# Eight ScalarE split copies put behind attention's exponentials, and a norm broadcast put into an earlier matmul group, in a two-layer decoder trunk

## The chip, the cores and the metric

The kernel runs on one core of a Trainium2 chip. The metric is the device time in microseconds (us) of one execution. The profile page and the trace describe one execution of their own; its time stands beside its span in the table below.

## The reference

The kernel computes two identical layers over 512 tokens of width 1024, in float32. Cut to what the change touches:

```python
def hybrid_layer(x, ...):                       # DEPTH = 2, SEQ = 512, D_MODEL = 1024
    h = rmsnorm(x, norm_mix)                    # one factor per token, then a gain per column
    z = h @ w_in
    q_a, k_a, v_a, q_m, k_m, v_m, o_m, if_m, gates = jnp.split(z, splits, axis=-1)
    # branch A: 8 query heads over 2 key heads of 64, blocks of 128 queries, window 128
    q_a, k_a = rope(rmsnorm(q_a)), rope(rmsnorm(k_a))
    att = sliding_window_attention(q_a, k_a, v_a, att_sinks)
    # branch B: mLSTM, 4 heads, q and k of 64, v of 128, in chunks, with running maximum
    hm = sigmoid(o_m) * rmsnorm(mlstm_chunkwise(q_m, k_m, v_m, i_pre, f_pre))
    mixed = sigmoid(gA) * (att @ w_att_branch) + sigmoid(gB) * (hm @ w_m_branch)
    x = x + mixed @ w_out
    u = relu(rmsnorm(x, norm_ffn) @ w_ff1)
    return x + (u * u) @ w_ff2
```

## The kernel before

**Matmuls.** Every large product is made of three matmuls (`mm3`, L47 issues each): an operand is split into a high part `h` and a low part `l`, and `h*h`, `h*l` and `l*h` are added in PSUM. Activations (`i` in the trace) are split once. Weights come in chunks of 128 x 512: a DMA on SP's queue into one of three raw buffers (`w`), a ScalarE copy into `wh` (L192), a VectorE subtraction into `wl` (L193), in four buffers each. A *group* is 512 output columns: 8 chunks (the depth 1024) times 4 blocks of 128 times 3 matmuls, 96 in all, into four PSUM banks, `mm`, which come as two pairs (blocks 0 and 1; blocks 2 and 3) out of six banks that go round. After its last chunk a group is evacuated out of PSUM, bank by bank. The matmuls of 128x128 on 128x512 that read `i` and `wh` or `wl` are "group matmuls" below.

**The remaining two banks**, `aux`, serve all small matmuls one after the other: transposes (L51), attention's scores and outputs (L47), and the broadcast of the norm factor. A small matmul that needs an `aux` bank can start when the readers of that bank's previous contents are done.

**The order.** `weave(fill, side)` writes a program order: `fill` is a list of matmul steps, a group being 8 units wide, and each entry of `side` is a function that is called at a place in those units. A scheduler then orders the instructions of each engine, by priority and by when it believes them ready. Each engine runs its own instructions strictly in that order.

The mixer has two weaves. The first holds the group of attention's q (units 0 to 8) and that of k, v and the i and f logits (8 to 16, 264 columns wide, "the key group"). The second holds the mLSTM's q and k (0 to 8), two gate groups g0 and g1 (8 to 24, evacuated by L761, a VectorE multiplication by the norm row), the mLSTM's v (24 to 32), and others behind it. Attention hangs in it as eight *units* (query block, key head), numbered 0 to 7; unit n begins at 5.75 + 1.65 n. Each has:

- scores: two small groups of matmuls from `kT` and `t`, read by a ScalarE copy of the previous block's half (L653) and by VectorE (L654);
- softmax: VectorE's maximum (L665 to L668), four ScalarE exponentials (L671) and the one of the sink, `es` (L673), VectorE's sum, reciprocal and scaling (L674 to L676);
- the probabilities' turn: four transposes (L51), the split in ScalarE and VectorE (L204, L205), and two POOL masks of each half (L690, L692);
- the output: four matmuls `aux<-t,v`, a ScalarE copy (L704), two VectorE sums (L708), and the split of the result (L711, L712).

For every query block, `q_tr` turns q and splits it in four ScalarE copies (L632) and four VectorE subtractions (L633). The mLSTM's decay runs beside it: the transposes of `acol`, the scans (L525, L528), and the copies of `cm` (L533, L534).

**`qk_split`** (L728 and on) splits the mLSTM's q and k into high and low parts, eight calls at 12.5 + 1.4 n: a ScalarE copy of 64 x 512 (L732 in the profile), then for q a POOL cast and memset and a VectorE subtraction (L737), for k a VectorE subtraction (L740). The results (`m_q`, `m_ql`, `m_k`) are used by `m_weights`, behind the v group.

**`Norm.along`** makes the row of norm factors `row[0]`, 128 x 512, each factor over all partitions: four VectorE multiplications of the identity by a column (L329), one float32 matmul with a matrix of ones into an `aux` bank (`aux<-t,ones` in the trace), and a ScalarE copy (L333). `norm.columns` (at 6.9 of the first weave) makes the column; `along` is called at 1.5 of the second weave. The mLSTM's q and k are multiplied by the row when they are evacuated.

`tc.issue_after(X)` makes the scheduler place what stands inside it behind X.

Of the kernel before, what the change touches and what calls it, by code (L numbers as in the profile page):

```python
# [12 lines left out]
AF = mybir.ActivationFunctionType  # L13
# [22 lines left out]
def hybrid_kernel(ctx, tc, x, norm_mix, w_in, att_q_norm, att_k_norm, att_sinks, m_gate_bias,  # L36
# [3 lines left out]
    ve, sc, gp = nc.vector, nc.scalar, nc.gpsimd  # L40
# [32 lines left out]
    def slot(dt=F32, shape=(P, T)):  # L73
        return now["act"].tile(list(shape), dt, tag="a", name=nm("a"))
# [19 lines left out]
    def f32(ap):  # L94
        return ap.bitcast(F32)
# [19 lines left out]
    def gains(row, c0):  # L115
        n = row.shape[0]
        gps = aux([P, n])
        pe.transpose(gps, row, ident[:n, :n])
        ve.tensor_copy(gcol[:, c0:c0 + n], gps)

    def g_mix(l, k):
        return gcol[:, 8 * l + k:8 * l + k + 1]

    def g_ffn(l, k):
        return gcol[:, 16 + 8 * l + k:17 + 8 * l + k]
# [214 lines left out]
    norm = norm0 = Norm(lambda k: g_mix(0, k))  # L340
# [89 lines left out]
    def mixer(l, norm, late, order, phase):  # L430
# [24 lines left out]
        row = []  # L455
# [4 lines left out]
        def ev_kv(b, ps):  # L460
# [2 lines left out]
        weave(tok_steps(acts, wcols(C_Q, 512), ev_q, order=order)  # L463
              + tok_steps(acts, lambda k: [W[k * P:(k + 1) * P, C_K:C_K + 256],
                                           W[k * P:(k + 1) * P, C_IF:C_IF + 8]], ev_kv, width=264),
              late + [(6.9, norm.columns)])


        ig = sm([P, NB, MH], "ig", 1)
# [113 lines left out]
        last_exp = []  # L583
# [31 lines left out]
        def q_vec(b):  # L615
            rope(q_tok[b].rearrange("p (h d) -> p h d", d=HD), b, HQ)

        def q_tr(b):


            ps = aux()
            for j in range(4):
                pe.transpose(ps[:, j * P:(j + 1) * P], q_tok[b][:, j * P:(j + 1) * P], ident)
            for j in range(2):
                qT[b, j] = temp(F32R)
                t4 = qT[b, j].rearrange("p (n i t) -> p n i t", n=2, i=2)
                p4 = ps[:, 2 * j * P:2 * (j + 1) * P].rearrange("p (n t) -> p n t", n=2)
                for i in range(2):
                    r = slice(64 * i, 64 * i + 64)
                    o = slice(64 - 64 * i, 128 - 64 * i)  # L630
                    g = gcols[0][r, l:l + 1]
                    sc.activation(t4[r, :, i, :], p4[r], AF.Copy, scale=g)  # L632
                    ve.scalar_tensor_tensor(t4[o, :, i, :], p4[r], g, f32(t4[r, :, i, :]), op0=ALU.mult,  # L633
                                            op1=ALU.subtract)
# [93 lines left out]
        def qk_split(m, i):  # L728
            t = qk_raw[m]
            r, o = slice(64 * i, 64 * i + 64), slice(64 - 64 * i, 128 - 64 * i)  # L730
            d = slot(F32R)
            sc.activation(d[r], t[r], AF.Copy)  # L732
            if m < 2:
                gp.tensor_copy(d[o], f32(d[r]))
                low = slot(F32R)
                gp.memset(f32(low[o]), 0.0)
                ve.tensor_tensor(low[r], t[r], f32(d[r]), op=ALU.subtract)  # L737
                m_q[2 * m + i], m_ql[2 * m + i] = d, low
            else:
                ve.tensor_tensor(d[o], t[r], f32(d[r]), op=ALU.subtract)  # L740
                m_k[2 * (m - 2) + i] = d
# [27 lines left out]
        def ev_v(b, ps):  # L769
            if b == 0:  # L770
# [7 lines left out]
        side = [(0, lambda: q_vec(0)), (0, k_vec), (0, lambda: q_vec(1)),  # L778
                (first - 1.25, k_tr), (first - 1.75, lambda: q_tr(0))]
        for i, (b, kv) in enumerate(units):  # L780
# [6 lines left out]
            if kv == 0 and b + 1 < NB:  # L787
                if b + 2 < NB:
                    side.append((at + 1, lambda b=b: q_vec(b + 2)))
                side.append((at + 2 * apart - 1.75, lambda b=b: q_tr(b + 1)))  # L790
        side.append((1.5, lambda: row.append(norm.along())))
        side += [(8.45 + 3.0 * i, f) for i, f in enumerate((gating0, gating1, gating2, gating3))]
        side += [(12.5 + 1.4 * n, lambda n=n: qk_split(n // 2, n % 2)) for n in range(8)]
        g0, s0 = gate_steps(0)
        g1, s1 = gate_steps(1)
# [104 lines left out]
        norm = Norm(lambda k: g_ffn(l, k))  # L900
# [10 lines left out]
    def mlp(l, norm, late, phase):  # L911
# [355 lines left out]
        def go(i, s, n):  # L1267
# [16 lines left out]
    late = ([(0.75 + 0.9 * (k - 2), lambda k=k: norm.turn(k)) for k in range(2, KT)]  # L1284
            + [(6.5, lambda: gains(grow, 16))]
            + [(3.0 + 2.0 * j, lambda j=j: norm.squares(j)) for j in range(2)])
    order = None
    for l in range(DEPTH):
        with ExitStack() as phase:
            norm = mixer(l, norm, late, order, phase)  # L1290
        late = norm.steps(1, 1.5, 0.5)
        with ExitStack() as phase:
            norm = mlp(l, norm, late, phase)
        late = norm.steps(0, 1.5, 0.5) if norm else []
        order = LATE_FIRST
# [40 lines left out]
```

## Time and profile before

| | |
|---|---|
| median of 3 runs | 1312.2 us (1311.24 to 1312.83) |
| the profiled execution's own time | 1312.1 us |
| its span in the trace | 1310.4 us, mean granted TensorE clock 0.998 |
| TensorE (PE) | 1288.5 us busy, 98% of the span, 7126 matmuls |
| VectorE (DVE) | 961.9 us, 73% |
| ScalarE (ACT) | 771.2 us, 59% |
| GpSimd (POOL) | 214.6 us, 16% |
| DMA | 196.52 MB, 171 GB/s of HBM traffic over the span |

1.7 us of the profiled execution lie outside its span. Matmul durations overlap, since the next one starts while the last one drains: what a group matmul takes of TensorE is the distance of two starts, not the duration shown. In the timeline, an entry in square brackets is idle time of that engine just before the instruction, and what ended it; `x2` or `x4` joins equal instructions that follow each other.

### The profile page before, as it was taken

What the parts mean: (1) busy time and instruction counts of PE and PEld (TensorE: products, weight loads), DVE (VectorE), ACT (ScalarE), POOL (GpSimd) and SP (SyncE); (2) the same over time, 40 slices, a digit from 0 to 9 for tenths busy, and PEclk for the clock granted to TensorE, in tenths of its full rate; (3) what the DMA queues carried; (4) which work ended last, traced back from release to release, by engine and by line L of the source; (5) the groups of instructions that cost most, each with busy time, mean ns of one, the idle gap of its engine ahead of it and who ended that gap; (6) DMA issues with size and microseconds to landing.
All of it is one profiled execution on the core that took longest, in us unless ns stands there. A gap on an engine that the chain in (4) does not pass through costs nothing.

```text
span 1310.4 us, 19489 instructions
## 1 busy us (share of the span) xinstructions
PE 1288.5 (98%) x7126; PEld 1111.5 (85%) x7126; DVE 961.9 (73%) x1477; ACT 771.2 (59%) x1365; POOL 214.6 (16%) x303
## 2 busy tenths in 40 slices
PE   9999999999999999999999999999999999999998
PEld 7877788888899989999887777888888999999987
DVE  4689755466587897978946896645766888979786
ACT  5556755444475666667544667554444766666663
POOL 4502201100011122120014122011000111212100
PEclk9999999999999999999999999999999999999999
DMA  5322236738288999787313222367392799897743
GB/s 153 102 68 67 64 91 162 183 112 221 78 205 192 266 185 238 180 182 197 112 37 109 65 65 73 107 159 169 121 263 50 194 232 247 176 260 150 188 139 136
DMA packets 139169, 196.52 MB, mean 150 GB/s; under 512 B 10424, under 2 KB 76576, under 8 KB 139072
## 3 DMA queue, kind: packets, MB, share of 16 engines
q1 hardware_dynamic: 93040, 135.88, 33.6%
q0 software_dynamic: 37568, 44.17, 21.9%
q10 hardware_dynamic: 8464, 15.21, 3.8%
q8 instruction: 56, 0.92, 0.3%
q14 instruction: 41, 0.34, 0.1%
HBM read 193.14 MB, written 31.46 MB: 171 GB/s over the span
## 4 chain that ended last, share of the span: by engine, by line
PE 86%; DVE 6%; ACT 4%; DMA 2%; issue 2%; SPq 0%; ACTq 0%; DVEq 0%; POOLq 0%
PE mm L47 74%; PE aux L47 10%; PE aux L51 2%; DMA raw<-in_w_ff_dram 1%; ACT wh L192 1%; DVE wl L193 1%; DMA w<-in_w_in_dram 1%; ACT t L671 1%; DVE t L633 0%; DVE a L740 0%; DVE t L676 0%; ACT t L632 0%; DVE wl L942 0%; ACT wh L938 0%; DVE u L956 0%
## 5 line engine op out<-in xcount | busy, mean ns | idle before, releaser
L47 PE MATMUL mm<-i,wh 128*128 128x512 f32 (+1 forms) x1216 | 329.8, 357 | 0.0
L938 ACT ACTIVATE wh<-raw 128x1024 fp32r<-128x1024 f32 x218 | 229.4, 1056 | 136.0 <-PE mm L47 68.2
L942 DVE TENSOR_TENSOR wl<-raw,wh 128x1024 fp32r<-128x1024 f32 x218 | 264.4, 1221 | 59.7 <-ACT wh L938 58.3
L193 DVE TENSOR_TENSOR wl<-w,wh 128x512 fp32r<-128x512 f32 (+1 forms) x208 | 140.1, 675 | 128.8 <-ACT wh L192 121.0
L47 PEld LDWEIGHTS mm<-i,wh 128*128 128x128 f32 x1216 | 210.5, 190 | 25.9 <-issue 0.5
L192 ACT ACTIVATE wh<-w 128x512 fp32r<-128x512 f32 (+1 forms) x208 | 127.0, 612 | 149.0 <-PE mm L47 122.9
L47 PE MATMUL mm<-i,wl 128*128 128x512 f32 (+1 forms) x608 | 214.3, 352 | 0.0
L47 PE MATMUL mm<-wh,uh 128*128 128x512 f32 x448 | 175.0, 391 | 0.0
L47 PE MATMUL mm<-wl,uh 128*128 128x512 f32 x448 | 174.7, 390 | 0.0
L47 PE MATMUL mm<-wh,ul 128*128 128x512 f32 x448 | 174.3, 389 | 0.0
L982 POOL DMA_DIRECT2D raw<-in_w_ff_dram x56 | 72.7, 1298 | 496.2 <-DVE wl L942 326.5
L47 PE MATMUL mm<-wh,i 128*128 128x512 f32 (+1 forms) x512 | 149.2, 368 | 1.0 <-ACT wh L192 0.7
L47 PEld LDWEIGHTS mm<-i,wl 128*128 128x128 f32 x608 | 115.4, 190 | 15.4 <-issue 0.5
L47 PE MATMUL mm<-hs,wh 128*128 128x256 f32 x672 | 122.2, 283 | 0.7 <-ACT u L1173 0.7
L47 PEld LDWEIGHTS mm<-hs,wh 128*128 128x128 f32 x672 | 105.7, 192 | 2.2 <-ACT u L1173 1.1
L47 PEld LDWEIGHTS mm<-wh,i 128*128 128x128 f32 x512 | 91.7, 188 | 17.1 <-DVE i L208 1.1
L47 PEld LDWEIGHTS mm<-wh,ul 128*128 128x128 f32 x448 | 84.1, 188 | 17.8
L47 PEld LDWEIGHTS mm<-wh,uh 128*128 128x128 f32 x448 | 84.3, 188 | 16.5
L47 PEld LDWEIGHTS mm<-wl,uh 128*128 128x128 f32 x448 | 84.2, 188 | 16.0
L47 PE MATMUL mm<-hs,wl 128*128 128x256 f32 x336 | 95.1, 283 | 0.0
L47 PE MATMUL mm<-wl,i 128*128 128x512 f32 (+1 forms) x256 | 93.1, 364 | 0.0
L996 DVE SCALAR_TENSOR_TENSOR x<-mm,ninv,x 128x512 f32<-128x512 f32 x112 | 81.0, 745 | 10.2 <-PE mm L47 10.0
(245 smaller groups left out, 2164.5 us busy)
## 6 DMA issues: line engine op xcount, KB each, us to landing
raw<-in_w_ff_dram SPq DMA_DIRECT2D x124, 512.0 KB, 5.9
w<-in_w_in_dram SPq DMA_DIRECT2D x128, 256.0 KB, 2.7
raw<-in_w_ff_dram POOLq DMA_DIRECT2D x56, 512.0 KB, 7.7
sum<-in_w_ff_dram ACTq DMA_DIRECT2D x28, 512.0 KB, 5.3
raw<-sum SPq DMA_DIRECT2D x28, 512.0 KB, 4.3
sum<-in_w_ff_dram POOLq DMA_DIRECT2D x20, 512.0 KB, 6.3
w<-in_w_out_dram SPq DMA_DIRECT2D x32, 256.0 KB, 3.3
w<-in_w_att_branch_dram SPq DMA_DIRECT2D x16, 256.0 KB, 2.6
```

The lines of the kernel that those rows point to most:

```text
L47: return nc.tensor.matmul(*args, **kw)
L51: return nc.tensor.transpose(*args)
L192: last_wh[:] = sc.activation(wh[:, :off], raw[:, :off], AF.Copy), wh
L193: ve.tensor_tensor(wl[:, :off], raw[:, :off], f32(wh[:, :off]), op=ALU.subtract)
L671: sc.activation(s3[:, i, :], s3[:, i, :], AF.Exp, bias=m[:, i:i + 1], accum_out=den[:, i:i + 1])
L938: last_wh[:] = sc.activation(hi, r, AF.Copy), hi[:, 0, :]
L942: ve.tensor_tensor(lo, r, f32(hi), op=ALU.subtract)
L982: nc.gpsimd.dma_start(r, w1_block(k, n, c0), accum_op=ALU.add)
L996: ve.scalar_tensor_tensor(xh[:, i, :], ps[i], norm.inv[:, 0 if sign > 0 else 1, b:b + 1], xh[:, i, :], op0=ALU.mult, op1=ALU.add)
```

## The change

Two edits. The call of `norm.along` moves from place 1.5 of the second weave to place 12.0 of the first, half way through the key group. And each ScalarE copy of `qk_split` is placed behind the `es` exponential of the attention unit whose softmax stands last before it in program order: the splits 0 to 7 behind units 3, 4, 5, 5 and later ones. Lines from L733 on have a number one higher in the changed kernel (L732 becomes L733, L737 L738, L761 L762).

```diff
         weave(tok_steps(acts, wcols(C_Q, 512), ev_q, order=order)
               + tok_steps(acts, lambda k: [W[k * P:(k + 1) * P, C_K:C_K + 256],
                                            W[k * P:(k + 1) * P, C_IF:C_IF + 8]], ev_kv, width=264),
-              late + [(6.9, norm.columns)])
+              late + [(6.9, norm.columns), (12.0, lambda: row.append(norm.along()))])
...
             d = slot(F32R)
-            sc.activation(d[r], t[r], AF.Copy)
+            with tc.issue_after(last_exp[0].ins):
+                sc.activation(d[r], t[r], AF.Copy)
...
-        side.append((1.5, lambda: row.append(norm.along())))
```

What a scheduler makes of that is seen in the order of the instructions, which is the same in both layers; the places below are layer 0's. In the names, the last number tells one tile from another.

TensorE: the norm broadcast, which stood inside the mLSTM's q and k group, stands behind the fourth chunk of the key group.

ScalarE, at the second `q_tr` (its four L632 write t_870 and t_875), before:

```order
L632 ACTIVATE t_174_870<-aux_173_865,gc0_103 64x2x128
L732 ACTIVATE a_238_1171<-a_177_892 64x512
L732 ACTIVATE a_253_1249<-a_177_892 64x512
L632 ACTIVATE t_175_875<-aux_173_865,gc0_103 64x2x128
L732 ACTIVATE a_277_1357<-a_178_894 64x512
L192 ACTIVATE wh_229_1138<-w_228_1136 128x512
L632 ACTIVATE t_175_875<-aux_173_865,gc0_103 64x2x128
L653 ACTIVATE t_195_961<-aux_196_962 128x256
```

And now:

```order
L632 ACTIVATE t_174_870<-aux_173_865,gc0_103 64x2x128
L632 ACTIVATE t_175_875<-aux_173_865,gc0_103 64x2x128 x2
L192 ACTIVATE wh_229_1138<-w_228_1136 128x512
L653 ACTIVATE t_195_961<-aux_196_962 128x256
L671 ACTIVATE t_112_631,den_191_940<-t_112_631,m_189_935 128x128 x4
```

The three split copies have left this place; with them a VectorE subtraction (L737) left from between L675 and L676 and a POOL cast. The copies stand later now, each behind an L673.

VectorE, at the evacuation of gate group g0 (a_1392 to a_1398 out of its four banks), before:

```order
L708 TENSOR_TENSOR t_245_1196<-aux_243_1192,t_244_1195 64x256
L193 TENSOR_TENSOR wl_322_1530<-w_320_1527,wh_321_1529 128x512
L761 TENSOR_TENSOR a_286_1392<-mm_181_900,t_143_694 128x512
L761 TENSOR_TENSOR a_287_1394<-mm_182_901,t_143_694 128x512
L761 TENSOR_TENSOR a_288_1396<-mm_186_924,t_143_694 128x512
L761 TENSOR_TENSOR a_289_1398<-mm_187_925,t_143_694 128x512
```

And now:

```order
L654 COPY_PREDICATED t_279_1366<-tri_l_79,aux_280_1367 128x256
L665 TENSOR_REDUCE m_274_1340<-t_255_1255 128x4
L666 SCALAR_TENSOR_TENSOR m_274_1340<-m_274_1340,nsinks_117 128x4
L668 TENSOR_TENSOR es_275_1343<-sinks_92,m_274_1340 128x4
L205 TENSOR_TENSOR t_283_1383<-aux_281_1377,t_282_1382 128x512
L762 TENSOR_TENSOR a_286_1392<-mm_181_900,t_72_502 128x512
L762 TENSOR_TENSOR a_287_1394<-mm_182_901,t_72_502 128x512
```

The evacuation has moved behind the maximum of unit 5 and the split of unit 4's probabilities (t_1383), some thirty VectorE instructions later.

TensorE, at the first use of g1's second pair of banks (mm_1428 and mm_1429, the banks that g0's blocks 0 and 1 held; mm_1400 and mm_1401 are its first pair), before:

```order
L47 MATMUL mm_291_1401<-i_5_153,wh_293_1404 128x512
L47 MATMUL mm_291_1401<-i_6_154,wh_293_1404 128x512
L47 MATMUL mm_291_1401<-i_5_153,wl_294_1405 128x512
L47 MATMUL mm_298_1428<-i_5_153,wh_293_1404 128x512
L47 MATMUL mm_298_1428<-i_6_154,wh_293_1404 128x512
```

And now:

```order
L47 MATMUL aux_273_1333<-kT_107_623,t_211_1040 128x256 x4
L47 MATMUL aux_280_1367<-kT_107_623,t_251_1239 128x256 x4
L51 MATMUL aux_281_1377<-ident_71,t_231_1148 128x128 x4
L47 MATMUL aux_295_1414<-t_261_1277,v2_108_624 128x512
L47 MATMUL aux_295_1414<-t_262_1278,v2_108_624 128x512
L47 MATMUL aux_295_1414<-t_263_1281,v2_108_624 128x512
L47 MATMUL aux_295_1414<-t_264_1282,v2_108_624 128x512
L47 MATMUL aux_302_1442<-kT_107_623,t_251_1239 128x256 x4
L47 MATMUL mm_298_1428<-i_5_153,wh_293_1404 128x512
```

Before, mm_1428 stood right behind the first six matmuls of g1. Now eight small groups stand ahead of it with hardly a group matmul among them: the transposes of t_1045, those of `acol`, the output aux_1307, and the five groups shown. Between the transposes of t_1045 and the end of aux_1442 lay 23 group matmuls; now three do. From the kernel's start, 421 group matmuls stood ahead of the transposes of t_1045 and 405 do now, 444 stood ahead of aux_1442's end and 408 do now; at the first `aux<-cm,sel` of the mLSTM both orders have 528, and they agree from there.

## The prediction

> **What bounds the kernel now.** I read the page's first and fourth parts, then TensorE's waits, then the timeline around each.
>
> ```profile
> span 1310.4 us, 19489 instructions
> PE 1288.5 (98%) x7126; PEld 1111.5 (85%) x7126; DVE 961.9 (73%) x1477; ACT 771.2 (59%) x1365; POOL 214.6 (16%) x303
> PE 86%; DVE 6%; ACT 4%; DMA 2%; issue 2%; SPq 0%; ACTq 0%; DVEq 0%; POOLq 0%
> ```
>
> TensorE is busy 98% of the span and makes up 86% of the chain that ended last. The change neither adds nor removes a matmul. So the time can change only by what TensorE idles, and by the clock that it is granted. The waits say where it idles ("engine, what it issues, what it waited for: us in all, times, longest"):
>
> ```profile
> PE aux L47 <- ACT t L632: 4.9, 2, 2.4
> PE aux L51 <- DVE t L654: 3.1, 4, 1.3
> PE aux L47 <- DVE rqk L276: 2.8, 2, 1.5
> ```
>
> The three largest groups, one stall per layer each (the second with small ones beside), are 10.8 us in all, 0.8% of the span. The first and third are the change's own places: L632 is `q_tr`, and the wait put down to L276 stands before the norm broadcast, whose VectorE operand is late. The sum is made against the profiled execution, 1312.1 us, 0.1 below the median of the three runs.
>
> **Part A: the norm broadcast goes into the key group.**
>
> ```profile
> 51.84 1.10 PE L47 MATMUL aux<-t,ones 128*128 128x512 f32 x2 [1.47 <-DVE rqk L276]
> 52.37 0.79 PE L47 MATMUL mm<-i,wh 128*128 128x512 f32 x1
> 65.14 0.30 PE L47 MATMUL aux<-kT,t 128*128 128x128 f32 x1 [0.32 <-DVE t L633]
> 701.59 1.10 PE L47 MATMUL aux<-t,ones 128*128 128x512 f32 x2 [1.30 <-DVE rqk L276]
> ```
>
> TensorE waits 1.47 us for it in layer 0 and 1.30 in layer 1. At its new place the column of factors is done, four chunks earlier, and no row of mine puts anything late behind it, so both stalls go. The matmul itself only moves. But the key group then ends later by the matmul's own time (51.84 to 52.37 shows 0.53 us, with its ramp some 0.9), and so do its evacuation, the ropes and the turn of k. The first user of those already waits 0.32 at 65.14; I give back 0.15. Its VectorE and ScalarE instructions (L329, L333) move to a stretch where neither is waited for. Ends: 0 if the delay all comes back at 65.14, 1.63 with the gap's edge. I take the stall itself, since the ropes have 13 us until 65.14: -1.4 in layer 0 and -1.3 in layer 1, **-2.7**.
>
> **Part B: three copies leave the second `q_tr`.** TensorE's timeline (layer 0, then layer 1's stall), ScalarE's, and VectorE's of layer 0:
>
> ```profile
> 76.69 0.40 PE L47 MATMUL mm<-i,wl 128*128 128x512 f32 x1
> 79.51 0.79 PE L47 MATMUL aux<-kT,t 128*128 128x256 f32 x4 [2.43 <-ACT t L632]
> ...
> 729.27 0.71 PE L47 MATMUL aux<-kT,t 128*128 128x256 f32 x4 [2.43 <-ACT t L632]
> ```
>
> ```profile
> 75.52 1.28 ACT L732 ACTIVATE a<-a 64x512 fp32r<-64x512 f32 x2
> 76.83 0.47 ACT L632 ACTIVATE t<-aux,gc 64x256 fp32r<-64x256 f32 x1
> 78.93 0.47 ACT L632 ACTIVATE t<-aux,gc 64x256 fp32r<-64x256 f32 x1 [0.59 <-DVE t L633]
> ```
>
> ```profile
> 75.74 0.49 DVE L633 SCALAR_TENSOR_TENSOR t<-aux,gc,t 64x256 fp32r<-64x256 f32 x1
> 76.36 1.01 DVE L737 TENSOR_TENSOR a<-a,a 64x512 fp32r<-64x512 f32 x1
> 77.29 1.09 DVE L676 TENSOR_TENSOR t<-t,den 128x512 f32<-128x512 f32 x1
> 78.42 0.48 DVE L633 SCALAR_TENSOR_TENSOR t<-aux,gc,t 64x256 fp32r<-64x256 f32 x1
> 78.92 0.44 DVE L654 COPY_PREDICATED t<-tri_l,aux 128x256 f32<-128x256 int32 x1
> ...
> 86.66 0.69 DVE L676 TENSOR_TENSOR t<-t,den 128x512 f32<-128x512 f32 x1
> ```
>
> The score matmul of 79.51 needs the bank that VectorE's L654 empties; L654 ends at 79.36, 0.15 before. The wait is put down to the L632 that ends at 79.40, but that one writes the half of q that this matmul doesn't read, and it waits for VectorE itself. So the path is VectorE's: L633 (to 76.23), L675, L737 (1.01), L676 (1.09), L633, L654. With the copies gone, L737 goes too, and L676 falls to the 0.69 it takes elsewhere. The path is then 76.23 + 0.2 + 0.69 + 0.48 + 0.44 = 78.05, and the matmul starts at 78.2 instead of 79.51: the stall falls from 2.43 to about 1.1. The Trainium skill, "GPSIMD Engine Reference", section 1, says that GpSimd shares SBUF interfaces with VectorE and that two-operand VectorE instructions contend; the 1.09 against 0.69 agrees, and the sum needs only the two rows.
>
> What is late next: the unit's transposes use the other `aux` bank, which the fourth L633 empties, now behind L665 (0.69) and a weight subtraction. I get 80.15 for them, a new stall of 0.8. The small one that follows (0.22 and 0.23, below) goes. Net -1.0 per layer. Ends: -1.9 if the transposes don't wait, and 0 if ScalarE's weight copy before that subtraction is late.
>
> Layer 0 has one cost more. After its stall the granted clock, third number from the end, was 0.57 over four us; layer 1, with the same 2.43 us, kept 1.00:
>
> ```profile
> 79.50:83.50 4.00, 3.99 (x15) 3.35 (x16) 3.62 (x8) 0.56 (x2) 0.00 (x0) 0.57 0.25 68
> 729.20:733.20 4.00, 3.93 (x20) 3.13 (x21) 3.88 (x9) 1.72 (x5) 0.00 (x0) 1.00 0.24 66
> ```
>
> ```profile
> 93.94 0.63 PE L51 MATMUL aux<-ident,t 128*128 128x128 f32 x4 [0.22 <-DVE t L654]
> ...
> 742.48 0.63 PE L51 MATMUL aux<-ident,t 128*128 128x128 f32 x4 [0.23 <-DVE t L654]
> ```
>
> From the score matmul to the next marked row are 14.43 us in layer 0 (93.94 - 79.51) and 13.21 in layer 1: the half clock cost 1.2. With two stalls of about one us I take it as gone. Part B: -2.2 in layer 0 and -1.0 in layer 1, **-3.2**.
>
> The Trainium skill, "TensorE: Matmul & The Clock Gate", section "What's actually happening", ties half clock to an idle window of some 3.4 us that runs freely. By it a shorter stall costs no clock, and R2 below would have no cause; the sum is the same. The 0.57 after 2.43 us speaks against reading the window as a threshold; that the window runs freely would let one layer fall in it and the other not, as the two rows show.
>
> **Part C: from those transposes to unit 4's output** (93.94 to 117.76). The copies, each 0.63 us of ScalarE, now stand between attention's own steps, and L738 between L676 and L708. Against this the 1.31 us stall at 117.76 (row below) shrinks, because fewer group matmuls and shorter VectorE queues stand ahead. Walking the three orders with the durations of these rows I get several new stalls of 0.2 to 0.5 that make up for it: **0**, with 1 us to either side per layer.
>
> **Part D: the evacuation of g0 moves back.**
>
> TensorE's timeline, then ScalarE's, VectorE's, and the window of the group matmuls alone (its length, then busy time and count):
>
> ```profile
> 117.76 0.63 PE L51 MATMUL aux<-ident,t 128*128 128x128 f32 x4 [1.31 <-DVE t L654]
> 120.31 1.16 PE L47 MATMUL aux<-t,v 128*128 128x512 f32 x4
> 124.15 0.71 PE L47 MATMUL aux<-kT,t 128*128 128x256 f32 x4 [0.63 <-DVE t L708]
> 129.30 0.62 PE L47 MATMUL mm<-i,wh 128*128 128x512 f32 x2
> 129.99 0.62 PE L47 MATMUL mm<-i,wh 128*128 128x512 f32 x2
> ```
>
> ```profile
> 118.42 0.60 ACT L204 ACTIVATE t<-aux 128x512 fp32r<-128x512 f32 x1 [0.20 <-PE aux L51]
> 121.51 0.59 ACT L704 ACTIVATE t<-aux 64x512 f32<-64x512 f32 x1 [2.48 <-PE aux L47]
> 125.18 0.61 ACT L533 ACTIVATE cm<-t 4x512 fp32r<-4x512 f32 x1
> ```
>
> ```profile
> 105.45 2.47 DVE L761 TENSOR_TENSOR a<-mm,t 128x512 f32<-128x512 f32 x4
> 119.47 0.69 DVE L205 TENSOR_TENSOR t<-aux,t 128x512 fp32r<-128x512 f32 x1
> 123.59 0.42 DVE L708 TENSOR_TENSOR t<-aux,t 64x256 f32<-64x256 f32 x1
> 125.92 0.68 DVE L534 TENSOR_TENSOR cm<-t,cm 4x512 fp32r<-4x512 f32 x1
> 126.63 0.69 DVE L665 TENSOR_REDUCE m<-t 128x4 f32<-128x512 f32 x1
> ```
>
> ```profile
> 117.70:129.28 11.58, 6.53 (x23) 1.00 0.22 66
> ```
>
> Before, the evacuation was over at 107.9, and in the stretch from 117.76 to 129.30, 11.54 us, 23 group matmuls (the last row, for those alone) filled TensorE between the small groups, which wait for one another through two banks. Now g1's second half has no bank until the evacuation, which VectorE reaches only behind L205 of unit 4. Three group matmuls are left in the stretch, and the small groups follow at their own pace:
>
> - transposes of t_1045 to the output: 0.66 + L204 0.60 + L205 0.69 + 0.14 (the 0.15 of part B) = 2.1.
> - output to scores: 1.20 + L704 0.59 + two L708 and a scan (1.25) + 0.14 = 3.2.
> - scores to the next transposes, through L533 and L534, which now stand ahead of L653 and L654: 0.5 + 0.61 + 0.68 + 0.44 and hand-overs = 2.4.
> - transposes to the last scores, through L665 (0.69), L666, L668 and L205: 2.1.
> - last scores and the first evacuation: 0.6.
>
> Together 10.4 us. A group matmul takes 0.23 (129.30 to 129.99 holds three). The stretch is 1.1 shorter and holds 20 fewer, 4.6 us of work: TensorE idles 3.5 more. **+3.5** per layer, +7.0. Ends: +1.5, if the wait for L533 is short because the scans run ahead (ScalarE and VectorE have no weight work here), to +5 with half clock. Behind it four weight copies stand in a row on ScalarE, each 0.6 us, for chunks needed 2.8 us apart (12 matmuls): hidden.
>
> **Part E: behind it** the 36 group matmuls that are still to be made up lie in long runs, which small groups interrupt without a wait that I find: 0. The split results are first used by `m_weights`, behind the v group; by my walk the last copy is then some 15 us old (an estimate), so its lateness is paid by nobody. POOL, 16% busy, makes its casts later without a reader that waits.
>
> **Sum:** -2.7 - 3.2 + 0 + 7.0 + 0 = +1.1, so 1312.1 + 1.1 = 1313.2 us.
>
> **Rivals.** 0.2% (2.6 us) is about what a measurement here can tell from no change.
>
> R1, faster: the bank wait of part D costs +1.5 per layer, its low end. The sum is then -2.9 and the time 1309.2. For it: no weight work lies in the stretch, and L533 waits for scans that have no other reader. Against: each hop is a chain of rows with no slack. It decides where part D stays under +1.7 per layer. Chance 0.24.
>
> R2, slower: the same stretch brings half clock. TensorE idles 4 us of 10 there, with single waits near 2; layer 0's 1.2 us after 2.43 is the row for it, layer 1's 0 the row against. In both layers, +2.4 gives 1315.6; it decides from 0.8 per layer on. Chance 0.31.
>
> R3, slower by another way: the splits come too late for the mLSTM. It needs 15 us of slack to vanish; with 3 us lost in each layer, 1318. Chance 0.03.
>
> That the change does nothing is excluded by the order; that its two gains and its loss cancel is my forecast.
>
> **How the numbers follow.** Forecast (losses and gains within 2.6 us): 0.42, 1313.2 us. R1 0.24, R2 0.31, R3 0.03. Faster 0.24, same 0.42, slower 0.34. The range: parts A, B and C can each be 1 to 2 us off, D by 2 per layer down and 1.5 up; 1308.5 to 1317.5 leaves out the sum of all low ends (1305) and R3. The forecast's own range is 1309.6 to 1314.8.
>
> **What would show it.** After: no wait before `aux<-t,ones`; stalls of about 1.1 and 0.8 where 2.43 stood; no half clock near 80; a stretch of about 10 us with three group matmuls and some 4 us of idle TensorE, ended by L708, L654 and L205, in each layer. I am wrong if that stretch idles under 2 us, if the clock falls in it, or if new waits stand behind it.

## The result, and the profile after

The changed kernel takes 1320.0 us in the median of 4 runs (1318.21 to 1320.95), the one before 1311.89 beside it: ratio 1.0061, 95% interval 1.0047 to 1.0074. It is slower by 8 us, where 1313.2 was forecast and 1317.5 was the upper end. The profiled execution took 1320.12.

The first lines of the page, the chain's shares, and what TensorE waited for:

```profile
span 1318.4 us, 19495 instructions
PE 1293.7 (98%) x7126; PEld 1115.1 (85%) x7126; DVE 962.7 (73%) x1477; ACT 772.3 (59%) x1365; POOL 221.3 (17%) x303
PE 85%; DVE 5%; issue 4%; ACT 3%; DMA 2%; POOL 1%; SPq 0%; ACTq 0%; POOLq 0%; DVEq 0%
```

```profile
PE aux L47 <- DVE t L708: 4.2, 2, 2.1
PE aux L51 <- DVE t L654: 3.1, 6, 1.1
PE aux L47 <- ACT t L632: 2.5, 2, 1.2
PE aux L47 <- POOL t L692: 2.3, 4, 0.9
PE aux L51 <- DVE t L708: 2.2, 4, 0.7
```

The wait for the norm broadcast is gone, and that for L632 is halved. New is one of 2.1 us per layer on L708. TensorE is "busy" 5 us longer with the same 7126 matmuls: a first sign that some of them ran slowly.

The stretch of part D in TensorE's timeline, layer 0:

```profile
111.64 0.63 PE L51 MATMUL aux<-ident,t 128*128 128x128 f32 x4 [0.33 <-DVE t L654]
...
113.83 1.15 PE L47 MATMUL aux<-t,v 128*128 128x512 f32 x4 [0.43 <-POOL t L690]
117.10 1.33 PE L47 MATMUL aux<-kT,t 128*128 128x256 f32 x8 [2.12 <-DVE t L708]
119.55 1.12 PE L51 MATMUL aux<-ident,t 128*128 128x128 f32 x4 [1.12 <-DVE t L654]
120.32 2.06 PE L47 MATMUL aux<-t,v 128*128 128x512 f32 x4
122.21 1.23 PE L47 MATMUL aux<-kT,t 128*128 128x256 f32 x4
123.23 1.05 PE L47 MATMUL mm<-i,wh 128*128 128x512 f32 x2
```

This is the pile of small groups that the order showed. It ends with g0's evacuation, which VectorE starts 16.6 us later than before (105.45):

```profile
122.07 2.47 DVE L762 TENSOR_TENSOR a<-mm,t 128x512 f32<-128x512 f32 x4
```

From 119.55 to about 125.4, TensorE takes double: four transposes 1.12 us where they took 0.63, two group matmuls 1.05 where they took 0.62. The windows of both layers (length, PE's busy time and count, granted clock, DMA):

```profile
118.50:125.40 6.90, 5.85 (x18) 0.51 0.01 2
770.50:777.40 6.90, 6.07 (x20) 0.51 0.01 2
```

Half clock, for about 6.8 us, in each layer.

### The profile page after: what moved, and what is told of

Its sections match the earlier page's. It is cut to its first block, busy times and chain, and to the rows that moved or that the text cites. A ratio compares the mean times of both kernels' runs of the same rounds, so it can differ in the third digit from the quotient of the medians.

```text
span 1318.4 us, 19495 instructions
## 1 busy us (share of the span) xinstructions
PE 1293.7 (98%) x7126; PEld 1115.1 (85%) x7126; DVE 962.7 (73%) x1477; ACT 772.3 (59%) x1365; POOL 221.3 (17%) x303
## 4 chain that ended last, share of the span: by engine, by line
PE 85%; DVE 5%; issue 4%; ACT 3%; DMA 2%; POOL 1%; SPq 0%; ACTq 0%; POOLq 0%; DVEq 0%
PE mm L47 72%; PE aux L47 11%; PE aux L51 2%; DMA raw<-in_w_ff_dram 2%; DVE wl L193 1%; ACT t L671 1%; DMA w<-in_w_in_dram 1%; DVE t L633 1%; ACT wh L192 1%; DVE t L676 0%; DVE t L708 0%; DVE t L654 0%; POOL t L692 0%; POOL t L690 0%; ACT wh L938 0%
## 5 line engine op out<-in xcount | busy, mean ns | idle before, releaser
L193 DVE TENSOR_TENSOR wl<-w,wh 128x512 fp32r<-128x512 f32 (+1 forms) x208 | 143.1, 688 | 137.2 <-ACT wh L192 131.0
L996 DVE SCALAR_TENSOR_TENSOR x<-mm,ninv,x 128x512 f32<-128x512 f32 x112 | 80.8, 744 | 10.3 <-PE mm L47 10.0
```

The lines of the kernel that those rows point to most:

```text
L193: ve.tensor_tensor(wl[:, :off], raw[:, :off], f32(wh[:, :off]), op=ALU.subtract)
L996: ve.scalar_tensor_tensor(xh[:, i, :], ps[i], norm.inv[:, 0 if sign > 0 else 1, b:b + 1], xh[:, i, :], op0=ALU.mult, op1=ALU.add)
```

## The experiments

The runs of the kernel before beside these had medians of 1312.0 to 1312.1 us. Theory 1 is that g0's late evacuation makes the whole loss, and that the tie of split 2 alone causes it.

**1. The broadcast alone.**

```diff
-            with tc.issue_after(last_exp[0].ins):
-                sc.activation(d[r], t[r], AF.Copy)
+            sc.activation(d[r], t[r], AF.Copy)
```

> The norm broadcast in the key group, the split copies left untied as before. Theory 1 (the whole loss comes from gate group g0's late evacuation, which the tie of split 2 alone causes, and from the half clock behind it): the two stalls of 1.47 and 1.30 us go, 1309.2 us. Theory 2 (the eight copies, standing between attention's own steps, hold up its chain everywhere): the same 1309.2. Theory 3 (the broadcast's new place delays the key group and all behind it): 1312 or more.

Measured 1309.33 us, ratio 0.9981 (0.9972 to 0.9989): -2.8 us. Theory 3 falls: the broadcast's new place costs nothing that shows, and its two stalls are won.

**2. The ties alone.**

```diff
-              late + [(6.9, norm.columns), (12.0, lambda: row.append(norm.along()))])
+              late + [(6.9, norm.columns)])
...
+        side.append((1.5, lambda: row.append(norm.along())))
```

> The copies tied as in the changed kernel, the norm broadcast left at its old place. Theories 1 and 2: the loss without part A's gain, 1320.0 + 2.7 = 1322.7 us. Theory 3: about 1312.

Measured 1321.49, ratio 1.0074 (1.0062 to 1.0087). The loss is the ties', whatever the broadcast does.

**3. All eight ties, split 2 called behind g0's evacuation.**

```diff
-        side += [(12.5 + 1.4 * n, lambda n=n: qk_split(n // 2, n % 2)) for n in range(8)]
+        side += [((12.5, 13.9, 16.1, 16.7, 18.1, 19.5, 20.9, 22.3)[n], lambda n=n: qk_split(n // 2, n % 2)) for n in range(8)]
```

> The changed kernel, every copy tied to the same exponential as there, but split 2 is called at 16.1 instead of 15.3, behind g0's evacuation in program order (n from 3 on keeps its place). The evacuation then stands ahead of unit 5 again, and g1's second half starts before the small groups pile up. Theory 1: A -2.7, B about -1.6 (as the trace after shows), nothing lost: 1307.5 us, no half clock near 118 us. Theory 2: the copies stand where they stood, so 1316 or more.

Measured 1310.74, ratio 0.9992 (0.9983 to 1.0001). Most of the loss is gone, with every copy tied to the same exponential as before. In VectorE's order, equal neighbours joined, the evacuation is row 156 there, 152 in the kernel before and 181 in the changed one. Theory 2 (the copies between attention's steps) falls. But 1307.5 was expected; 3 us of gain are missing.

**4. Only split 2 tied, and the broadcast moved.**

```diff
-            with tc.issue_after(last_exp[0].ins):
+            with ExitStack() as order:
+                if 2 * m + i == 2:
+                    order.enter_context(tc.issue_after(last_exp[0].ins))
                 sc.activation(d[r], t[r], AF.Copy)
```

> The norm broadcast in the key group and one tie only, split 2 behind unit 5's exponential; the other seven copies untied, as before. Theory 1: part D's 4.6 us and some 2 us behind it in each layer, less A's 2.7: 1322 us, with half clock near 120 us. Theory 2: one copy of eight is moved: 1310 us.

Measured 1317.49, ratio 1.0047 (1.0034 to 1.0059): one tie costs 8.2 us against experiment 1. The place looks as in the changed kernel, the 2.12 us wait and the double durations included:

```profile
118.27 2.05 PE L47 MATMUL aux<-kT,t 128*128 128x256 f32 x8 [2.12 <-DVE t L708]
120.72 1.12 PE L51 MATMUL aux<-ident,t 128*128 128x128 f32 x4 [0.40 <-DVE t L654]
```

The sign is theory 1's; the size is less than the 13 expected. Experiment 9 shows a part of the difference; the rest stays open.

**5. TensorE's idle time filled.** 14 matmuls per layer, each multiplying zeros of the selection matrix into g1's first bank (cut to the new matmuls; other lines of the edit note the three instructions they are tied to and call `warm` at 19.9):

```diff
...
+        def warm():
+            for key, n in ((("out", 1, 0), 9), (("scores", 3, 0, 0), 4), (("turn", 2, 0), 1)):
+                with tc.issue_after(last_pe[key].ins):
+                    for _ in range(n):
+                        pe.matmul(g1_ps[0], sel[64:128, 0, :], acts[0][0][64:128], start=False, stop=False)
...
```

> The changed kernel with 14 more matmuls per layer that add zero (half of the rows, zeros from the selection matrix) to g1's first bank, put where TensorE idles between the small groups: 9 behind the output aux_1307, 4 behind the scores aux_1367, 1 behind the next output. The order is otherwise the changed kernel's. Theory 1a (the half clock behind the idle stretch is 2.0 to 2.9 us per layer of the loss): no granted clock under 0.9 near 120 and 773, 1315 us (1314 to 1316). Rival (the small groups' chain hides the clock, only the idle counts): 1320 us or a little more.

Measured 1317.79, ratio 1.0046 (1.0033 to 1.0059): 2.2 us under the changed kernel, with more work. The timeline and a window of that place:

```profile
112.98 1.17 PE L47 MATMUL aux<-t,v 128*128 128x512 f32 x4 [0.42 <-POOL t L692]
114.07 2.33 PE L47 MATMUL mm<-i,sel 64*128 64x512 f32 x9
116.34 1.26 PE L47 MATMUL aux<-kT,t 128*128 128x256 f32 x8
117.53 1.21 PE L47 MATMUL mm<-i,sel 64*128 64x512 f32 x4
118.72 0.66 PE L51 MATMUL aux<-ident,t 128*128 128x128 f32 x4
119.14 1.16 PE L47 MATMUL aux<-t,v 128*128 128x512 f32 x4
...
121.52 0.73 PE L47 MATMUL mm<-i,wh 128*128 128x512 f32 x2
```

```profile
114.00:126.00 12.00, 11.80 (x55) 1.00 0.01 1
```

The clock stays at 1.00, and counted from the transposes of t_1045 no small group of the stretch starts more than 0.1 us later than in the changed kernel. So the idle time caused the half clock, and the half clock's exposed part is 2.2 us (about 1 per layer), not the 4 to 6 that I expected. The intervals of the two ratios overlap, so the medians alone would be a weak ground; the traces agree with them: from attention's first scores in the second weave to the first `aux<-cm,sel`, the changed kernel takes 97.03 us in layer 0 and 96.74 in layer 1, and this one 96.06 and 95.77. The rest of what the clock slowed presumably lay beside VectorE's waits. The rest of the loss is there at full clock.

**6. Splits 3 to 7 tied, 0 to 2 free.** The condition is `2 * m + i > 2`.

> The norm broadcast in the key group; splits 0 to 2 untied as before, splits 3 to 7 tied. Experiment 3 lies 1.4 us over experiment 1 though its second q_tr stall is 1.2 us shorter in each layer. Theory 1b (the last splits, whose VectorE subtractions L741 then stand beside unit 7's split and g1's evacuation, hold up the last outputs by 0.6 and 1.4 us in each layer): 1312 us, with waits on L692 near 153. Rival (the first copies, between attention's own steps, cost it): 1309.3 us as experiment 1.

Measured 1308.82, ratio 0.9975 (0.9966 to 0.9984): the rival. Waits on L692 are there (0.39 and 0.88 us in layer 0), but others shrink; alone, these five ties cost nothing.

**7. As 3, with only splits 0 to 2 tied.** The condition is `2 * m + i < 3`.

> As experiment 3, but only splits 0 to 2 are tied; 3 to 7 are free. Theory 1b: the gain of the second q_tr without the loss at the end, 1307.5 us. Rival (the first copies cost it): 1310.7 us.

Measured 1305.72, ratio 0.9955 (0.9943 to 0.9967): the fastest, 6.3 us under the kernel before. The rival's 1310.7 falls too: the first copies cost nothing. So neither set costs by itself, and all eight do when split 2 is called later: 1310.74 against 1305.72. In experiment 3, VectorE's timeline at the end of attention shows how:

```profile
145.09 0.69 DVE L676 TENSOR_TENSOR t<-t,den 128x512 f32<-128x512 f32 x1
145.81 0.69 DVE L741 TENSOR_TENSOR a<-a,a 64x512 fp32r<-64x512 f32 x1
146.53 1.89 DVE L762 TENSOR_TENSOR a<-mm,t 128x512 f32<-128x512 f32 x3
148.33 0.83 DVE L708 TENSOR_TENSOR t<-aux,t 64x256 f32<-64x256 f32 x2
149.09 0.68 DVE L741 TENSOR_TENSOR a<-a,a 64x512 fp32r<-64x512 f32 x1
...
151.26 0.68 DVE L205 TENSOR_TENSOR t<-aux,t 128x512 fp32r<-128x512 f32 x1
```

Between unit 7's scaled probabilities (L676) and their split (L205) stand two split subtractions and g1's evacuation; its masks and output then wait, 0.61 and 1.37 us on L692.

**8. As 7, split 2 free as well.** The condition is `2 * m + i < 2`.

> As experiment 7 with split 2 untied as well. It isn't ahead of the second q_tr any more, since it is called later. Theory 1b: 1307.5 us; rival: 1310 us.

Measured 1307.48, ratio 0.997 (0.9958 to 0.9981), theory 1b's number, though experiment 6 leaves it without its reason.

**9. The changed kernel with ties 0 to 2 only.** The condition is `2 * m + i < 3`, split 2 at its old place, so g0's evacuation stays late.

> The changed kernel with the ties of splits 3 to 7 taken away; split 2 is tied at its old place, so g0's evacuation stays late. Part D and its half clock stay. Theory 4 (part E's loss, some 2 us per layer, comes from splits 3 to 7, whose subtractions and g1's evacuation stand ahead of unit 7's split on VectorE once the first three are tied too): 1316 us. Rival (part E's loss follows from the idle stretch alone, which leaves the last units too few group matmuls to hide behind): 1320 us.

Measured 1318.19, ratio 1.0045 (1.0032 to 1.0057): 1.8 us of the changed kernel's loss goes, half way between the two expectations. The 2.12 us wait is there as in the changed kernel, and half clock behind it.

**10. The changed kernel without one of its eight ties.** The condition is `2 * m + i != 2`.

> The changed kernel with one tie taken away, split 2's. Theory 1: the evacuation comes early again, as in experiment 3: 1310.7 us, no half clock near 118 us. If the other seven ties had a part of their own in the loss beside the combination seen in experiment 3: 1313 or more.

Measured 1306.17, ratio 0.9956 (0.9942 to 0.997): below the kernel before by 6 us, and below the changed kernel by 13.8. TensorE's timeline of the stretch, shortened, and its window:

```profile
114.59 0.63 PE L51 MATMUL aux<-ident,t 128*128 128x128 f32 x4 [0.31 <-DVE t L633]
...
119.94 0.63 PE L47 MATMUL aux<-kT,t 128*128 128x256 f32 x4
120.40 0.39 PE L47 MATMUL mm<-i,wl 128*128 128x512 f32 x1
120.63 0.40 PE L47 MATMUL mm<-i,wh 128*128 128x512 f32 x1
120.87 0.64 PE L47 MATMUL aux<-kT,t 128*128 128x256 f32 x4
...
124.44 0.63 PE L47 MATMUL aux<-kT,t 128*128 128x256 f32 x4
```

```profile
114.59:124.91 10.32, 10.21 (x56) 1.00 0.29 78
```

The same eight small groups, in 10.3 us, with group matmuls between them: 0.1 us idle. VectorE has g0's evacuation early again:

```profile
108.25 2.48 DVE L764 TENSOR_TENSOR a<-mm,t 128x512 f32<-128x512 f32 x4
```

With experiment 3, where the tie stays and the evacuation goes ahead of the split, this settles the cause. Beside the other seven, the tie of split 2 is worth 13.8 us (alone, in experiment 4, 8.2); the other seven bring 3.2 (1309.33 - 1306.17). In experiment 3, which keeps this tie too but calls the split later, 4.6 us of that gain are missing; which of the later subtractions' places does it there wasn't tried one by one.

## Why the prediction was wrong, by its steps

**Part A, -2.7:** right. Experiment 1 measured -2.8, and the stalls are gone; what came back at the first scores (0.44 us where 0.32 stood, in experiment 1) is of the size given.

**Parts B and C, -3.2 and 0:** right. Experiment 10 against 1, the seven harmless ties, is -3.2. In the traces, from attention's first scores in the second weave to the transposes that follow the second `q_tr` (92.08 us in experiment 1, 90.42 in experiment 10; 346 group matmuls stand ahead of them in both orders), experiment 10 is 2.1 us shorter in layer 0 and 1.1 in layer 1, where B had 2.2 and 1.0. From there to the first `aux<-cm,sel` it is 0.2 and 0.1 longer, where C had 0. The stalls themselves came out at 1.23 for 1.1 and 0.43 for 0.8, and the small one that was to go stayed (0.26), here of experiment 10:

```profile
77.04 0.71 PE L47 MATMUL aux<-kT,t 128*128 128x256 f32 x4 [1.23 <-ACT t L632]
78.88 0.66 PE L51 MATMUL aux<-ident,t 128*128 128x128 f32 x4 [0.43 <-DVE t L633]
```

**Part D, +7.0, and part E, 0:** here the sum failed. Freeing split 2 is worth 13.8 us, 6.9 per layer, where D and E together had 3.5. D's mechanism was right, and against the kernel before so was its size: the order had shown it, and a walk of the hops gave 10.4 us for the stretch, which took 10.74 at full clock (110.78 to 121.52 in experiment 5). With 20 fewer matmuls the stretch of the kernel before would take 6.97 us (11.54 - 4.57), so this part is 3.8 per layer, near the 3.5. Two things that stood in the sum at nothing come on top. The half clock: 2.2 us over both layers by experiment 5. What lies behind the stretch: experiment 5, at full clock, needs 38.22 us from the first group matmul behind the stretch's last scores (aux_1442) to the first `aux<-cm,sel`; before, it was 27.76, and 36 more group matmuls make 8.2 us of difference, which leaves 2.3 per layer. Part E had that at nothing, "without a wait that I find". Of these 2.3, some 0.9 go with the ties of splits 3 to 7 (experiment 9). Together, 2 x 3.8 + 2.2 + 2 x 2.3 = 14.4, against the 13.8 measured.

That division depends on the kernel one compares with. Experiment 10 differs from the changed kernel by the one tie. Its stretch holds 23 group matmuls in 10.32 us, and the part behind it takes 28.86 us (124.91 to 153.77) with 37 group matmuls fewer than experiment 5's. Against it the stretch loses 5.0 per layer, the part behind it 0.9 and the clock 1.0, together the 6.9 that were measured. What holds either way: D's 3.5 was not the whole, and half clock and the part behind the stretch, both at nothing in the sum, were paid. Two of the prediction's own signs of being wrong came: the clock fell in the stretch, and new waits stood behind it.

The part behind the stretch wasn't separated further; the waits there are many and small:

```profile
128.50 0.71 PE L47 MATMUL aux<-kT,t 128*128 128x256 f32 x4 [0.57 <-DVE t L710]
137.13 0.63 PE L51 MATMUL aux<-ident,t 128*128 128x128 f32 x4 [0.42 <-DVE t L710]
144.45 0.63 PE L51 MATMUL aux<-ident,t 128*128 128x128 f32 x4 [0.24 <-ACT t L706]
150.69 0.50 PE L47 MATMUL aux<-t,v 128*128 128x512 f32 x1 [0.30 <-POOL t L694]
152.77 0.96 PE L47 MATMUL aux<-t,v 128*128 128x512 f32 x3 [0.88 <-POOL t L694]
```

These (experiment 5, whose lines are two higher) are 2.4 us per layer where the kernel before had 1.1 in small ones. Last, the range: R2, half clock in both layers, came true almost at its price (2.2 for 2.4). Its 1315.6 was taken as a case beside the others, with part E's nothing and part D's middle in it; together with E's 2.3 per layer (2 x 2.3 = 4.6) it reaches 1320.2. The range joined the bounds of D and the clock, but gave E none upward.

**R1** falls: the bank wait was not cheap. **R3** falls as a cause: in experiment 3 the splits are as late as in the changed kernel and most of the loss is gone, and freeing split 2 alone, with the other seven as late, restores the time.

## What to carry to other kernels

A tie that holds back one small copy can hold back whatever the scheduler places behind it in program order: look for where evacuations of PSUM went, not only where the tied instruction went. One tie of eight turned a gain of 6 us into a loss of 8. And when a reordering takes the filler out of a chain of small matmuls, three bills come: the idle time, the clock behind it, and the tail of the chain, which then runs with its partners in another order; a walk that stops at the end of the stretch sees the first.

## What the hardware showed

I had taken two waits, each near the 2.4 us that had cost half clock in one layer and nothing in the other, for a matter of chance. Around a wait of 2.12 us, with smaller ones on either side, the clock fell in both layers of the changed kernel, and at the same place in both layers of experiments 2, 4 and 9. It didn't fall at the same moment: in layer 0 of experiment 4 it fell inside the wait of 2.12 us, which ends at 118.27, and in layer 1 only behind the score matmuls that follow that wait, near 772.8. Here both moments, then the whole half clock of either layer:

```profile
117.00:118.00 1.00, 0.00 (x0) 0.73 0.00 0
772.00:773.00 1.00, 0.14 (x2) 0.91 0.00 0
117.40:124.40 7.00, 5.73 (x21) 0.51 0.00 0
772.80:776.30 3.50, 3.05 (x10) 0.51 0.00 0
```

Half clock lasts about 6.8 us in the one and 3.4 in the other. These two lengths are the only ones in the eight layers: the long one in five (both of the changed kernel and of experiment 9, layer 0 of experiment 4), the short one in three. And shorter waits can be enough. In layer 0 of experiment 3 waits of 1.21 and 0.43 us at the second `q_tr`, 1.4 us of matmuls apart, were followed by half clock, where I took it as gone; with the same two waits it stayed away in layer 1, and in experiment 10. So the length of a single wait doesn't decide it. The window of experiment 3:

```profile
79.10:82.60 3.50, 3.50 (x11) 0.51 0.28 77
```

With the gaps filled, in experiment 5, it stayed at 1.00. The Trainium skill, "TensorE: Matmul & The Clock Gate", section "Why this matters for your kernels", warns of idle gaps over about 3 us; here none was that long, and shorter ones with little work between were enough.
